# Two blocks on one core: small fp32 products of attention and scan in other groups, bias rows built early, four gate pairs as plain products

## The chip, the cores and the metric

One core of a Trainium2 chip runs the whole program in one launch. The metric is the time of one execution in device microseconds, as the median of several runs. The kernel before took 2028.05 us (three runs: 2022.07, 2028.05 and 2031.63 us). Matrix products run on TensorE (PE in the views, PEld is its weight load), elementwise work on VectorE (DVE) and ScalarE (ACT), small work and one DMA queue on GpSimd (POOL); most transfers are issued by SyncE (SP). Each engine works off its own instructions strictly in the order in which they were laid down.

## What is computed

A sequence of 1024 tokens of width 1024 passes through two blocks; everything is float32. Cut to what the change touches:

```python
h = rmsnorm(x, norm_mix_pre)
q, k, v, u, g_attn, g_ssm = split(h @ w_in)          # 512, 128, 128, 512, 1024, 1024
logits = q·k / 8 + bias[dist]                        # 8 query heads, 2 kv heads, blocks of 128
p = softmax over 256 keys and one sink               # the block itself and the one before it
y_attn = (p @ v) @ w_attn_branch
z = gelu(s5_ssm(u, lam, log_dt, b, c, d_skip))       # 32 groups of 16 channels, 64 complex states
z = z * sigmoid(z @ w_glu);  y_ssm = z @ w_ssm_branch
merged = sigmoid(g_attn) * y_attn + sigmoid(g_ssm) * y_ssm
x = x + rmsnorm(merged @ w_out)
x = x + rmsnorm(square(relu(rmsnorm(x) @ w_ff_in)) @ w_ff_out)
...
```

The lines left out are a second block with three branches and a last norm; the change does not touch its code.

## The kernel before

**Large products.** A float32 matrix is held as two float16 parts (`split`, L135 on ACT for the high part, L136 on DVE for the low part), and a product takes three float16 matmuls per slice of the contraction. Two column tiles of 128 are made at a time, a "pair". `strassen` makes a pair by seven products of 12 matmuls of 512 columns (L208 to L210), with four differences (`tw`, L164) and seven splits of weights ahead of it and an evacuation of one ACT copy (L226), two sums into `u` (L231, L237) and three into `c` or a destination (L253). `first_pair` makes a pair plainly: 96 matmuls (L383), four splits of weights, and an evacuation straight from PSUM. Weights come by SP in blocks `raw` of 512 KB (L145, three buffers) and are split into a pool of `NW` = 15 pairs of weight tiles `whi`/`wlo`.

**Order.** The program is written as units, each with a preparation (loads and splits of its weights) that is started some units earlier. A list scheduler of the framework lays the instructions of all units out on each engine by dependences and priorities. The order is fixed when the program is built.

**Startup.** Eight tiles of x are squared and summed on ACT (L540), the reciprocal root comes by way of DVE (L426) and POOL (L428, `rs`), DVE makes the normed rows `h` (L541), PE transposes them (`tr`, L448), and the transposed tiles are split. `first_pair` for k and v (`pq`) starts on the first tokens while later tiles are still on the way (its first half is cut in two pieces of 256 columns); the pair for the first half of q follows, then a `strassen` pair for the second half.

**Bias.** A unit behind the `strassen` pair of q (L573 to L592) multiplies a one-hot table with the copied bias table by eight fp32 matmuls `pbias` (K = 33, all 128 output rows alike, L586), copies them to 128 partitions, writes them to DRAM (`bdr`, 1.5 MB, L589) and reads them back with a row pitch one element short (L591), which gives each row its shift.

**Attention.** For each block of 128 tokens `attend` makes the logits `lg` (L773), a fused sum and maximum on DVE (L775), the exponentials on ACT (L784) and the scaling on DVE; `values` transposes the probabilities (`pt`, L800), copies them, and multiplies by v (`pvo`, L807: per block four groups, each of two matmuls with 256 columns that fill one half of the output rows). A fp32 matmul is two records in the trace.

**Scan.** For each of four groups of channels (`uc`) `ssm_tables` builds tables: `pwk` (L921, 16 output rows), one ACT copy of 16x512 for each half, DMAs by POOL, `pg` transposes (L934). `ssm_scan` makes the states `S` (L944), the scan on DVE, and the output `py`: for each half `a` and each `r` one product with K = 128 (L969) and then two with K = 64 (L971). The scan's u goes through DRAM (`udr`) into 16 partitions at a time by eight POOL DMAs of 256 KB (L985). Pairs of the two gates, GA and GS, are laid beside attention and scan as filler for PE.

**Parameters of the scan** (L625 to L757) are many small DVE operations on temporaries in the memory of the arena from 92 to 108 KB, which also holds the transposed tiles in float32 (`K32`).

Of the kernel before, what the change touches and what calls it, by code (L numbers as in the profile page):

```python
# [16 lines left out]
P = 128  # L17
T = 1024
D = 1024
H = 512  # L20
# [30 lines left out]
def kernel(ctx: ExitStack, tc: tile.TileContext, I: dict, out: bass.AP):  # L51
# [8 lines left out]
    R = 152  # L60
    NW, NQ = 15, 12
# [273 lines left out]
    def linear2(W, c0, act, cb, scale, early=None):  # L335
# [3 lines left out]
        def prepare():  # L339
            raw = load_k(W, lambda w: w.rearrange("(k p) n -> p k n", p=P), c0)  # L340
            for c in range(2):
                ws.append(hl_tile())
                split(*ws[c], raw[:, :, c * P:(c + 1) * P], SW)
# [180 lines left out]
    a21_1 = Flat(144)  # L524
    g_pre = A32(140, D)
    K32 = [A32(92 + 8 * q, 4 * H).rearrange("p (k t) -> p k t", k=4) for q in range(4)]

    @do
    def _():
        xin = [A32((72, 56)[t // 4] + 4 * (t % 4), D) for t in range(NT)]  # L530
        for t in range(NT):
# [3 lines left out]
            if t == 1:  # L535
                prepare(1)
# [22 lines left out]
    bias_t = A32(84, 8 * 256).rearrange("p (h s) -> p h s", h=8)  # L559
    sink = small([P, 8], "sink")  # L560

    @do
    def _():
        nc.vector.tensor_copy(kk[0:64, 1, :], kk[64:128, 0, :])
# [7 lines left out]

    @do  # L573
    def _():

        relb = small([33, 8], "relb")
        nc.vector.memset(relb, 1.0)
        nc.gpsimd.dma_start(out=relb[0:32, :], in_=I["rel_bias"])
        hot = A32(92, 384)[0:33, :]
        nc.gpsimd.dma_start(out=hot, in_=I["onehot"])  # L580
        relrep = A32(94, 8 * P)[0:33, :].rearrange("p (h m) -> p h m", h=8)
        nc.vector.tensor_copy(relrep, relb.unsqueeze(2).to_broadcast([33, 8, P]))
        vrow = A32(108, 8 * 384).rearrange("p (h i) -> p h i", h=8)
        for h in range(8):
            pb = aux("pbias")
            MM(pb[:, 0:384], relrep[:, h, :], hot, start=True, stop=True)  # L586
            nc.scalar.copy(vrow[:, h, :], pb[:, 0:384])
        bdr = pdr.tile([P, 8 * 384], F32, tag="bdr", name="bdr")
        nc.gpsimd.dma_start(out=bdr, in_=vrow.rearrange("p h i -> p (h i)"))  # L589
        skew = bass.AP(bdr.tensor, bdr.offset + 127, [[8 * 384 - 1, P], [384, 8], [1, 256]])  # L590
        nc.gpsimd.dma_start(out=bias_t, in_=skew)  # L591
        nc.gpsimd.dma_start(out=sink, in_=I["sinks"][0].partition_broadcast(P))  # L592
# [13 lines left out]
    toff = [92.0]  # L606

    def tmp(n):
        a = A32(toff[0], n)
        toff[0] += n * 4 / KB  # L610
        assert toff[0] <= 108
        return a
# [13 lines left out]
    def _():  # L626
        L16 = tmp(3 * P)[0:16, :].rearrange("p (i m) -> p i m", i=3)
# [8 lines left out]
        prm = tmp(48).rearrange("p (i r) -> p i r", i=3)  # L636
# [3 lines left out]
        def EXP(dst, src, n):  # L640
            save = toff[0]
# [15 lines left out]
        def SINCOS(sn, cs, y, n):  # L657
            save = toff[0]
# [34 lines left out]

        dt_ = small([P, 16], "dt")
# [13 lines left out]
        TT(Ai[:, 1, :], mags[:, 0, :], snd[:, 0, :], ALU.mult)  # L708
        for m in (1, 2, 4):
# [4 lines left out]
        nr, den, f_r, f_i, t1 = (tmp(16) for _ in range(5))  # L714
# [13 lines left out]
        braw = tmp(512).rearrange("p (i r c) -> p i r c", i=2, r=NP)  # L728
# [4 lines left out]
        tb1 = tmp(256).rearrange("p (r c) -> p r c", r=NP)  # L733
        tb2 = tmp(256).rearrange("p (r c) -> p r c", r=NP)
        cmul(Bf[:, 0], Bf[:, 1], frb, fib, braw[:, 0], braw[:, 1], tb1, tb2)
        for i, n_ in enumerate(("c_re", "c_im")):
            craw = tmp(256).rearrange("p (u q) -> p u q", u=4)
# [52 lines left out]
    def values(n):  # L790
        pr = Pb[n % 2]
        for kv in range(2):
            pv = aux("pvo")
            for par in range(2):
                pt = aux("pt")
                for i in range(2):
                    h = kv * 4 + par + 2 * i
                    for half in range(2):
# [192 lines left out]
    for c0 in range(0, 8, 2):  # L991
        gate_ahead(GS, c0)
# [533 lines left out]
```

## Time and profile before

| | before |
|---|---|
| median of three runs | 2028.05 us (2022.07 to 2031.63) |
| the profiled execution | 2025.8 us, its span 2024.1 us |
| PE busy | 1971.5 us (97%), 9536 matmuls |
| DVE busy | 1534.5 us (76%) |
| ACT busy | 875.8 us (43%) |
| POOL busy | 105.4 us (5%) |
| DMA | 171.80 MB, mean 85 GB/s |

The span is the time between the first and the last record; the execution's own time is 1.7 us above it. A matmul's busy time is modelled and overlaps with its neighbours: a matmul of 512 columns counts as about 380 ns though the next one starts 216 ns later. Gains on PE are therefore counted from one start to the next, which is what the timeline view gives. Idle time in the rows is put down to what ended it.

### The profile page before, as it was taken

What the parts mean: (1) busy time and instruction counts of PE and PEld (TensorE: products, weight loads), DVE (VectorE), ACT (ScalarE), POOL (GpSimd) and SP (SyncE); (2) the same over time, 40 slices, a digit from 0 to 9 for tenths busy, and PEclk for the clock granted to TensorE, in tenths of its full rate; (3) what the DMA queues carried; (4) which work ended last, traced back from release to release, by engine and by line L of the source; (5) the groups of instructions that cost most, each with busy time, mean ns of one, the idle gap of its engine ahead of it and who ended that gap; (6) DMA issues with size and microseconds to landing.
All of it is one profiled execution on the core that took longest, in us unless ns stands there. A gap on an engine that the chain in (4) does not pass through costs nothing. (4 is left out here: it accounts for less than half of the span.)

```text
span 2024.1 us, 25660 instructions
## 1 busy us (share of the span) xinstructions
PE 1971.5 (97%) x9536; PEld 938.3 (46%) x9536; DVE 1534.5 (76%) x2830; ACT 875.8 (43%) x1691; POOL 105.4 (5%) x157
## 2 busy tenths in 40 slices
PE   7999999999999999999999999999999999999998
PEld 5434445554454444444444444454444443444443
DVE  7687679877568966878876578589678896899942
ACT  7316643334246735625527445434333332344511
POOL 1000000110010000000000011000000011110000
PEclk9999999999999999999999999999999999999999
DMA  5231162577321221121122422211111121112222
GB/s 182 87 109 53 42 132 69 162 235 254 104 89 63 63 73 42 63 62 53 58 68 94 126 76 86 67 43 60 63 56 62 53 63 31 63 63 68 89 84 84
DMA packets 130574, 171.80 MB, mean 85 GB/s; under 512 B 12025, under 2 KB 98293, under 8 KB 130320
## 3 DMA queue, kind: packets, MB, share of 16 engines
q1 hardware_dynamic: 124736, 160.46, 24.4%
q0 software_dynamic: 3536, 8.64, 2.4%
q10 hardware_dynamic: 2176, 1.05, 0.3%
q8 instruction: 75, 1.23, 0.2%
q14 instruction: 51, 0.42, 0.1%
HBM read 138.01 MB, written 30.93 MB: 83 GB/s over the span
## 5 line engine op out<-in xcount | busy, mean ns | idle before, releaser
L208 PE MATMUL b<-arena,whi 128*128 128x512 f16 x2044 | 776.8, 380 | 9.1 <-ACT p L226 6.5
L209 PE MATMUL b<-arena,whi 128*128 128x512 f16 x2044 | 777.2, 380 | 0.9 <-DVE arena L136 0.9
L210 PE MATMUL b<-arena,wlo 128*128 128x512 f16 x2044 | 776.5, 380 | 0.0
L135 ACT ACTIVATE whi<-tw 128x512 f16<-128x512 f32 x292 | 172.9, 622 | 337.6 <-DVE tw L164 286.8
L209 PEld LDWEIGHTS <-whi 128*128 128x128 f16 x2044 | 200.5, 98 | 253.1 <-issue 19.8
L210 PEld LDWEIGHTS <-wlo 128*128 128x128 f16 x2044 | 200.5, 98 | 243.1 <-issue 7.6
L208 PEld LDWEIGHTS <-whi 128*128 128x128 f16 x2044 | 200.5, 98 | 242.6 <-issue 8.0
L253 DVE SCALAR_TENSOR_TENSOR c<-b,u 128x512 f32<-128x512 f32 x204 | 139.7, 686 | 109.9 <-PE b L210 109.6
L136 DVE SCALAR_TENSOR_TENSOR wlo<-tw,whi 128x512 f16<-128x512 f32 x292 | 194.2, 683 | 7.7 <-ACT whi L135 7.4
L136 DVE SCALAR_TENSOR_TENSOR wlo<-raw,whi 128x512 f16<-128x512 f32 (+1 forms) x261 | 176.7, 687 | 13.9 <-ACT whi L135 13.7
L415 PEld LDWEIGHTS <-arena 128*128 128x128 f16 x1152 | 112.7, 98 | 133.2
L135 ACT ACTIVATE whi<-raw 128x512 f16<-128x512 f32 (+1 forms) x261 | 151.2, 609 | 41.5 <-PE b L209 17.0
L164 DVE TENSOR_TENSOR tw<-raw,tw 128x512 f32<-128x512 f32 x134 | 91.8, 685 | 1.4 <-DMA raw<-in_w_in_dram 0.4
L843 ACT ACTIVATE c<-c 128x512 f32<-128x512 f32 x60 | 37.7, 629 | 116.6 <-DVE c L253 98.4
L354 PE MATMUL pl<-arena,whi 128*128 128x512 f16 x320 | 83.1, 379 | 2.2 <-DVE fetch L997 1.8
L415 PE MATMUL po<-arena 128*128 128x512 f16 x384 | 84.0, 379 | 0.0
L415 PE MATMUL pf<-arena 128*128 128x512 f16 x384 | 84.0, 379 | 0.0
L415 PE MATMUL pw<-arena 128*128 128x512 f16 x384 | 83.0, 379 | 0.0
L231 DVE SCALAR_TENSOR_TENSOR u<-b,p 128x512 f32<-128x512 f32 x79 | 54.0, 684 | 33.0 <-PE b L210 32.9
L383 PE MATMUL pq<-arena,whi 128*128 128x512 f16 (+1 forms) x288 | 79.0, 360 | 0.0
L237 DVE SCALAR_TENSOR_TENSOR u<-b,u 128x512 f32<-128x512 f32 x79 | 54.1, 685 | 17.6 <-PE b L210 17.5
L226 ACT ACTIVATE p<-b 128x512 f32<-128x512 f32 x79 | 46.0, 583 | 38.2 <-PE b L210 38.2
(326 smaller groups left out, 2175.5 us busy)
## 6 DMA issues: line engine op xcount, KB each, us to landing
raw<-in_w_in_dram SPq DMA_DIRECT2D x86, 512.0 KB, 3.5
raw<-in_w_ff_in_dram SPq DMA_DIRECT2D x32, 512.0 KB, 3.6
raw<-in_w_ff_out_dram SPq DMA_DIRECT2D x32, 512.0 KB, 3.5
fetch<-gdr SPq DMA_DIRECT2D x32, 256.0 KB, 4.2
xr<-xdr SPq DMA_DIRECT2D x32, 256.0 KB, 3.4
gdr<-c SPq DMA_DIRECT2D x24, 256.0 KB, 2.0
arena<-in_x_dram SPq DMA_DIRECT2D x8, 512.0 KB, 9.9
raw<-in_w_out_dram SPq DMA_DIRECT2D x8, 512.0 KB, 5.6
```

The costliest lines, as they stand in the source:

```text
L135: ACT(hi, src, AF.Copy, scale=scale)
L136: STT(lo, src, scale, hi, ALU.mult, ALU.subtract)
L164: TT(t, a, b, ALU.subtract)
L208: MM(b[:, 0:n], whi[:, k], act[0][:, i, k, sl], start=(first and k == 0), stop=False, skip_group_check=not first)
L209: MM(b[:, 0:n], whi[:, k], act[1][:, i, k, sl], start=False, stop=False, skip_group_check=not first)
L210: MM(b[:, 0:n], wlo[:, k], act[0][:, i, k, sl], start=False, stop=(k == nk - 1), skip_group_check=not first)
L231: STT(v["u2"], o2, scale, v["p1"], ALU.mult, ALU.add)
L237: STT(v["u3"], o, scale, v["u2"], ALU.mult, ALU.add)
L253: STT(d, vw(o), scale, vw(v[u]), ALU.mult, ALU.add)
L354: MM(bs[s], w[:, k], a[:, k, s * H:(s + 1) * H], start=(k == 0 and w is hi and a is act[0]), stop=(k == 3 and w is lo))
L383: MM(o, w[:, k % 4], a, start=(k == 0 and w is hi and a is ahi), stop=(k == 7 and w is lo))
L415: MM(bs[s], part(a), w[:, s * H:(s + 1) * H], start=(k == 0 and a is ahi and w is whi), stop=(k == nk - 1 and a is alo))
```

## The change

Six things change.

1. **Second gate.** The four pairs of GS are made by `first_pair` in place of `strassen`.
2. **Bias.** One `pbias` matmul with eight output rows takes the place of eight. Its unit becomes a function `bias_rows`, called in the startup behind the load of the second tile of x. The table goes to DRAM from 8 partitions, each row read 128 times (`to_broadcast`), and `bias_read` stands in the unit behind the k/v and q pairs.
3. **Room.** The arena grows from 152 to 160 KB, the weight tiles go from 15 to 11 pairs, and the temporaries of the scan's parameters move out of the memory of `K32`.
4. **values.** Per block four groups of four transposes, then four matmuls of 512 columns whose output rows alternate between the lower and the upper half, and one split of 128x512. The attention's output is ordered by kv head, so `linear2` loads `w_attn_branch` in two DMAs of 64 partitions.
5. **pwk.** The products go to four strips of 32 output rows in turn; four ACT copies of 16x128 take the place of one of 16x512.
6. **py.** All eight products with K = 128 come first, then sixteen with K = 64 that alternate between the row halves `a` = 0 and 1 and two PSUM banks.

```diff
-    R = 152
-    NW, NQ = 15, 12
+    R = 160
+    NW, NQ = 11, 12
...
+            if by_kv:
+                raw = pw.tile([P, 4, 256], F32, tag="raw", name=nm("raw"), bufs=3)
+                for a in range(2):
+                    nc.sync.dma_start(out=raw[64 * a:64 * a + 64],
+                                      in_=W[256 * a:256 * a + 256].rearrange("(k p) n -> p k n", p=64)[:, :, c0:c0 + 256])
...
+    def bias_rows():
...
+        hot, row = q2("hot"), q2("vrow")
+        nc.gpsimd.dma_start(out=hot[0:33, 0:384], in_=I["onehot"])
+        pb = aux("pbias")
+        MM(pb[0:8, 0:384], relb, hot[0:33, 0:384], start=True, stop=True)
+        nc.scalar.copy(row[0:8, 0:384], pb[0:8, 0:384])
+        nc.gpsimd.dma_start(out=bdr.rearrange("p (h i) -> h p i", h=8),
+                            in_=row[0:8, 0:384].unsqueeze(1).to_broadcast([8, P, 384]))
...
+    def bias_read():
+
+        skew = bass.AP(bdr.tensor, bdr.offset + 127, [[8 * 384 - 1, P], [384, 8], [1, 256]])
+        nc.gpsimd.dma_start(out=bias_t, in_=skew)
...
             if t == 1:
+                bias_rows()
                 prepare(1)
...
     @do
     def _():
+        bias_read()
         nc.vector.tensor_copy(kk[0:64, 1, :], kk[64:128, 0, :])
...
-    toff = [92.0]
...
+    toff = [131.0]
...
+        for half, kv in parts:
+            pt = aux("pt")
+            for i in range(4):
+                nc.tensor.transpose(pt[:, i * P:(i + 1) * P], pr[:, 4 * kv + i, half * P:(half + 1) * P], ident)
+            pts[half, kv] = A32(142 + 2 * (2 * half + kv), H)
+            nc.scalar.copy(pts[half, kv], pt)
+        pv = aux("pvo")
+        for half, kv in reversed(parts):
+            MM(pv[kv * 64:(kv + 1) * 64, :], vtok[:, n - 1 + half, kv * 64:(kv + 1) * 64], pts[half, kv],
+               start=(half == 1), stop=(half == parts[0][0]))
+        sl = (slice(None), slice(None), slice(n * P, (n + 1) * P))
+        split(at[0][sl], at[1][sl], v4(pv), SA)
...
+        if plain:
+            first_pair(w_in, col + c0 * P, hC, a21_1, cb, UNH)
...
+            for i in range(2):
+                for r in range(4):
+                    MM(pk[32 * r:32 * r + C, 0:P], Bf[rows, i, p0 + r, :],
+                       CA[rows, i, r, 0:8, :].rearrange("p d c -> p (d c)"), start=(i == 0), stop=(i == 1))
             for r in range(4):
-                for i in range(2):
-                    MM(pk[0:C, r * P:(r + 1) * P], Bf[rows, i, p0 + r, :],
-                       CA[rows, i, r, 0:8, :].rearrange("p d c -> p (d c)"), start=(i == 0), stop=(i == 1))
-            nc.scalar.copy(Wsb[:, :, a, :], pk[0:C, :].rearrange("p (r m) -> p r m", r=4))
+                nc.scalar.copy(Wsb[:, r, a, :], pk[32 * r:32 * r + C, 0:P])
...
+        for r in range(4):
+            for a in range(2):
+                MM(pys[a][:, cols_[r]], Kt[:, 2 * r + a, :], U[:, 2 * r + a, :], start=(r == 0), stop=False,
+                   skip_group_check=(r > 0))
+        for r in range(4):
+            for i in range(2):
+                for a in range(2):
+                    rows = slice(a * 64, (a + 1) * 64)
+                    MM(pys[a][:, cols_[r]], CA[rows, i, r, 1:9, :].rearrange("p d c -> p (d c)"), Ht[rows, i, r, :],
+                       start=False, stop=(i == 1), skip_group_check=(r > 0))
...
-        gate_ahead(GS, c0)
+        gate_ahead(GS, c0, True)
```

The units are written in another order at the startup, so the scheduler lays the engines' instructions out in another order there. On POOL the eight steps `rs` are the reciprocal roots of the eight tiles of x, in order. Before, behind the first of them:

```order
L428 TENSOR_TENSOR rs_24_141<-rs_24_141,mhalf_75 128x1
L428 TENSOR_TENSOR rs_28_163<-rs_28_163,mhalf_75 128x1
L428 TENSOR_TENSOR rs_32_185<-rs_32_185,mhalf_75 128x1
L428 TENSOR_TENSOR rs_36_207<-rs_36_207,mhalf_75 128x1
L428 TENSOR_TENSOR rs_40_229<-rs_40_229,mhalf_75 128x1
L428 TENSOR_TENSOR rs_44_251<-rs_44_251,mhalf_75 128x1
L428 TENSOR_TENSOR rs_48_273<-rs_48_273,mhalf_75 128x1
L746 DMA arena<-in_d_skip_dram 16x512
L580 DMA arena<-in_onehot_dram 33x384
```

And on POOL in the changed kernel, from the second tile's root on:

```order
L436 TENSOR_TENSOR rs_28_153<-rs_28_153,mhalf_75 128x1
L549 DMA bdr<-vrow_96 8x128x384
L436 TENSOR_TENSOR rs_32_175<-rs_32_175,mhalf_75 128x1
L436 TENSOR_TENSOR rs_36_197<-rs_36_197,mhalf_75 128x1
L556 DMA arena<-bdr 128x8x256
L436 TENSOR_TENSOR rs_40_219<-rs_40_219,mhalf_75 128x1
L436 TENSOR_TENSOR rs_44_241<-rs_44_241,mhalf_75 128x1
L436 TENSOR_TENSOR rs_48_263<-rs_48_263,mhalf_75 128x1
L436 TENSOR_TENSOR rs_52_285<-rs_52_285,mhalf_75 128x1
```

The write of `bdr` now stands between the roots of the second and the third tile, and its read back, which needs the write to have landed, in front of the roots of tiles five to eight.

On DVE, at the normed rows of the second and third tile (L541 before, L572 in the changed kernel), before:

```order
L541 SCALAR_TENSOR_TENSOR arena<-arena,rs_24_141 128x1024
L426 TENSOR_SCALAR rs_28_163<-ss_27_161 128x1
L541 SCALAR_TENSOR_TENSOR arena<-arena,rs_28_163 128x1024
L136 SCALAR_TENSOR_TENSOR arena<-tr_145,arena 128x4x128
L136 SCALAR_TENSOR_TENSOR arena<-tr_150,arena 128x4x128
L426 TENSOR_SCALAR rs_32_185<-ss_31_183 128x1
L541 SCALAR_TENSOR_TENSOR arena<-arena,rs_32_185 128x1024
```

And in the changed kernel, the last instructions up to the third tile's rows (`raw_477` to `raw_650` are the blocks of weights of the second half of q and of the pair behind it):

```order
L164 TENSOR_TENSOR tw_497<-raw_479,raw_477 128x512
L164 TENSOR_TENSOR tw_507<-raw_479,tw_487 128x512
L136 SCALAR_TENSOR_TENSOR wlo_490<-tw_487,whi_489 128x512
L136 SCALAR_TENSOR_TENSOR wlo_494<-tw_485,whi_493 128x512
L164 TENSOR_TENSOR tw_656<-raw_648 128x512
L164 TENSOR_TENSOR tw_658<-raw_650,tw_656 128x512
L164 TENSOR_TENSOR tw_668<-raw_650,raw_648 128x512
L164 TENSOR_TENSOR tw_678<-raw_650,tw_658 128x512
L572 SCALAR_TENSOR_TENSOR arena<-arena,rs_32_175 128x1024
L434 TENSOR_SCALAR rs_36_197<-ss_35_195 128x1
L572 SCALAR_TENSOR_TENSOR arena<-arena,rs_36_197 128x1024
```

The third tile's rows, and with them those of all later tiles, now stand behind work on six further blocks of weights, the last of which is the eighth block that the program loads.

On PE, the end of the eight products with K = 128 of the scan's output and the first of the others in the changed kernel (L981 has K = 128, L987 K = 64; before, one product of the first kind and two of the second alternated in one bank):

```order
L981 MATMUL py_2530<-arena 128x128
L981 MATMUL py_2531<-arena 128x128
L981 MATMUL py_2530<-arena 128x128
L981 MATMUL py_2531<-arena 128x128
L987 MATMUL py_2530<-arena 128x128
L987 MATMUL py_2531<-arena 128x128
L987 MATMUL py_2530<-arena 128x128
```

The products with K = 64 now follow one another in pairs that use different rows of the array and different banks.

## Rows read from the trace of the kernel before

**Rows 1.** The page: length of the span, busy time of PE and the others.
```profile
span 2024.1 us, 25660 instructions
...
PE 1971.5 (97%) x9536; PEld 938.3 (46%) x9536; DVE 1534.5 (76%) x2830; ACT 875.8 (43%) x1691; POOL 105.4 (5%) x157
```

**Rows 2.** Stretches: busy time and instructions of each engine, granted clock, DMA share.
```profile
core 0: us, PE busy (x) PEld busy (x) DVE busy (x) ACT busy (x) POOL busy (x), PEclk, DMA share, GB/s
50.00:100.00 50.00, 50.00 (x216) 23.29 (x214) 35.02 (x46) 19.21 (x31) 4.24 (x7) 0.93 0.27 90
90.00:100.00 10.00, 10.00 (x33) 4.27 (x32) 1.88 (x5) 2.03 (x4) 2.13 (x4) 0.67 0.39 159
...
200.00:250.00 50.00, 49.66 (x241) 25.07 (x241) 30.83 (x117) 28.18 (x83) 1.60 (x3) 1.00 0.10 34
...
350.00:400.00 50.00, 49.62 (x292) 29.70 (x291) 46.19 (x100) 18.90 (x35) 6.38 (x12) 1.00 0.59 158
...
1000.00:1050.00 50.00, 50.00 (x233) 22.69 (x232) 39.33 (x65) 13.31 (x25) 0.00 (x0) 1.00 0.21 63
```

**Rows 3.** Waits of PE: engine, line, waited for, us in total, times, longest.
```profile
PE tr L448 <- DVE arena L541: 13.9, 3, 7.9
...
PE lg L773 <- DVE m L775: 4.9, 2, 2.9
...
PE b L209 <- DVE arena L136: 0.9, 2, 0.4
```

**Rows 4.** Groups of PE by form: count | busy, mean ns | idle before.
```profile
L807 PE MATMUL pvo<-arena 128*64 128x256 f32 x120 | 32.8, 393 | 0.6
...
L921 PE MATMUL pwk<-arena 64*16 64x128 f32 x128 | 12.8, 270 | 0.0
...
L586 PE MATMUL pbias<-arena 33*128 33x384 f32 x16 | 6.9, 594 | 0.0
```

**Rows 5.** Timeline of PE in attention and scan: start, length of the run.
```profile
208.00 0.38 PE L209 MATMUL b<-arena,whi 128*128 128x512 f16 x1
208.21 0.38 PE L210 MATMUL b<-arena,wlo 128*128 128x512 f16 x1
208.52 1.08 PE L807 MATMUL pvo<-arena 128*64 128x256 f32 x4
209.53 0.39 PE L208 MATMUL b<-arena,whi 128*128 128x512 f16 x1
...
303.72 1.97 PE L944 MATMUL S<-arena 128*64 128x128 f32 x32
...
317.30 0.49 PE L969 MATMUL py<-arena 128*128 128x128 f32 x2
317.72 0.71 PE L971 MATMUL py<-arena 64*128 64x128 f32 x4
318.36 0.49 PE L969 MATMUL py<-arena 128*128 128x128 f32 x2
```

**Rows 6.** Costs on DVE: the page's groups of weight splits, differences and evacuations.
```profile
L253 DVE SCALAR_TENSOR_TENSOR c<-b,u 128x512 f32<-128x512 f32 x204 | 139.7, 686 | 109.9 <-PE b L210 109.6
...
L164 DVE TENSOR_TENSOR tw<-raw,tw 128x512 f32<-128x512 f32 x134 | 91.8, 685 | 1.4 <-DMA raw<-in_w_in_dram 0.4
```

**Rows 7.** Timeline of the startup on DVE, ACT and PE.
```profile
16.15 1.28 DVE L541 SCALAR_TENSOR_TENSOR arena<-arena,rs 128x1024 f32<-128x1024 f32 x1 [0.73 <-POOL rs L428]
...
12.82 1.05 ACT L540 ACTIVATE arena<-arena 128x1024 f32<-128x1024 f32 x1
...
35.81 0.59 PE L383 MATMUL pq<-arena,whi 128*128 128x512 f16 x2
```

**Rows 8.** DMA issues from 90 to 100 us: KB, us to landing.
```profile
bdr<-arena POOLq DMA_DIRECT2D x1, 1536.0 KB, 5.4
```

**Rows 9.** Waits of POOL.
```profile
POOL arena L591 <- DMA bdr<-arena: 4.6, 1, 4.6
```

**Rows 10.** DMA from 248 to 256 us: packets, the queue's share, issues with us to landing.
```profile
DMA packets 223, 0.78 MB, mean 98 GB/s; under 512 B 32, under 2 KB 32, under 8 KB 223
...
q0 software_dynamic: 223, 0.78, 84.6%
...
arena<-udr POOLq DMA_DIRECT2D x8, 256.0 KB, 12.0
raw<-in_w_in_dram SPq DMA_DIRECT2D x1, 512.0 KB, 21.3
```

**Rows 11.** The page's DMA issues: a block of weights over the whole program.
```profile
raw<-in_w_in_dram SPq DMA_DIRECT2D x86, 512.0 KB, 3.5
```

More of the change, by code (lines that the diff above doesn't have):

```diff
@@ L523 @@
     hC = COMB(0)
-    a21_1 = Flat(144)
+    a21_1 = Flat(152)
     g_pre = A32(140, D)
     K32 = [A32(92 + 8 * q, 4 * H).rearrange("p (k t) -> p k t", k=4) for q in range(4)]
+    bias_t = A32(84, 8 * 256).rearrange("p (h s) -> p h s", h=8)
+    sink = small([P, 8], "sink")
+    bdr = pdr.tile([P, 8 * 384], F32, tag="bdr", name="bdr")
+    def bias_rows():
+        relb = small([33, 8], "relb")
+        nc.vector.memset(relb, 1.0)
+        nc.gpsimd.dma_start(out=relb[0:32, :], in_=I["rel_bias"])
+        hot, row = q2("hot"), q2("vrow")
[5 more added lines that the diff above has]
+                            in_=row[0:8, 0:384].unsqueeze(1).to_broadcast([8, P, 384]))
+        nc.gpsimd.dma_start(out=sink, in_=I["sinks"][0].partition_broadcast(P))
+    def bias_read():
+        skew = bass.AP(bdr.tensor, bdr.offset + 127, [[8 * 384 - 1, P], [384, 8], [1, 256]])
+        nc.gpsimd.dma_start(out=bias_t, in_=skew)
     @do
@@ L571 @@
     strassen(w_in, 256, hC, nothing, UNH * 0.125, dest=lambda c, s, sl: q_t[:, 2 + c, s * H:(s + 1) * H])
[L573 to L592, printed above, removed]
     G, PS_, C = 32, 64, 16
@@ L605, with tmp @@
     mags = small([P, 2, 16], "mags")
-    toff = [92.0]
-    def tmp(n):
+    toff = [131.0]
+    def tmp(n, kb=None):
+        if kb is not None:
+            return A32(kb, n)
         a = A32(toff[0], n)
         toff[0] += n * 4 / KB
-        assert toff[0] <= 108
+        assert toff[0] <= 136
         return a
@@ L692, in SINCOS @@
             toff[0] = save
+        toff[0] = 135.0
         dt_ = small([P, 16], "dt")
@@ L708, in _ @@
         TT(Ai[:, 1, :], mags[:, 0, :], snd[:, 0, :], ALU.mult)
+        toff[0] = 131.0
         for m in (1, 2, 4):
@@ L713, in _ @@
                  Ar[:, m:m + 1, :].to_broadcast([P, m, 16]), Ai[:, m:m + 1, :].to_broadcast([P, m, 16]), t1, t2)
-        nr, den, f_r, f_i, t1 = (tmp(16) for _ in range(5))
+        toff[0] = 135.75
+        nr, den, f_r, f_i = (tmp(16) for _ in range(4))
+        t1 = tmp(16, 131)
         TS(nr, Ar[:, 1, :], -1.0, None, ALU.add)
@@ L791, in values @@
         pr = Pb[n % 2]
[L792 to L795, printed above, removed]
[L796 to L810 removed]
+        parts = [(half, kv) for half in range(0 if n else 1, 2) for kv in range(2)]
+        pts = {}
+        for half, kv in parts:
[10 more added lines that the diff above has]
+        split(at[0][sl], at[1][sl], v4(pv), SA)
     @do
@@ L963, in ssm_scan @@
         pys = [aux("py") for _ in range(2)]
[L964 to L972 removed]
+        cols_ = [slice(r * P, (r + 1) * P) for r in range(4)]
+        for r in range(4):
[8 more added lines that the diff above has]
+                       start=False, stop=(i == 1), skip_group_check=(r > 0))
+        for a in range(2):
             ACT(U.rearrange("p (r a) n -> p a r n", a=2)[:, a], pys[a].rearrange("p (r n) -> p r n", r=4),
```

51 lines of the change are left out of this document (15 added, 36 removed).

## The prediction

> **What bounds the kernel now.** I read the page first. PE is busy for 97% of the span [rows 1], so the time is PE's unless a stage shows otherwise. The table of stretches says where it is full: 216 to 233 instructions in 50 us where the matmuls have 512 columns, and 49.6 to 50 us busy also in attention (200 to 250 us) and scan (350 to 400 us) [rows 2]. There the count rises to 241 and 292: small fp32 products sit between the large ones. PE's waits are the third view: 4.9 us for the first logits, behind DVE, and 13.9 us for transposes at the startup, behind DVE's normed rows [rows 3]. So work taken from PE is time gained, if DVE and ACT keep up; the startup is the one stage in which PE waits for others.
>
> The sum is made against the profiled execution's 2025.8 us, which lies 2 us under the median of the runs. A difference under 0.5%, about 10 us, can't be told from none.
>
> **The bias product.** Eight matmuls become one. Their 16 records take 6.9 us [rows 4], in a stretch whose granted clock is 0.67, a mean of the two levels 1.2 and 2.4 GHz [rows 2]. Two records stay: **-6**.
>
> **values.** One group of four records takes PE from 208.52 to 209.53, 1.01 us, and its first record starts 0.31 us after the large matmul instead of 0.21 [rows 5]. Inside it, 256 columns take some 0.216 us a record, one after the other, since both matmuls use one half of the output rows. 120 records [rows 4] are 7.5 blocks of 16: 4.0 us a block. After, a block has 8 records of 512 columns, 0.43 us each, on alternating halves. What alternating halves do is seen at `S`: 32 records of 128 columns in 1.97 us with the tail, 62 ns each [rows 5], against 0.108 us for 128 columns alone (half the 0.216). Two run at a time. So 4 x 0.43 and a change, 1.9 us a block, 7.5 x 2.1 = **-16**. If they don't overlap it is -4.
>
> **pwk.** 128 records, 12.8 us [rows 4], 0.1 us each, so nothing overlaps now. Four strips of output rows take turns after. The nearest row is `S` with two halves: half the time, **-6**; between 0 and -9 (four at a time). The Trainium skill, "TensorEngine Tiling (Array Packing)", section "When to Use Tiling", has fourfold column tiling for 32 output rows. By it the term would be -9 and the sum 3 us lower; no row here has four strips. The added ACT copies (32 in place of 8, 128 columns each) lie beside PE: ACT is busy 19 of 50 us there [rows 2].
>
> **py.** One product with K = 128 and two with K = 64 take from 317.30 to 318.36, 1.06 us, for six records [rows 5]; of that 0.65 us would be six times 0.108, the rest are the two changes of tile shape. A `uc` has eight such, 8.5 us. After: 16 records at 0.108, 32 in pairs at 0.062, two changes at 0.1, 3.9 us. Four `uc` give **-18**; without overlap -12.
>
> **Fewer changes of shape elsewhere.** By the order of instructions PE changes between tile shapes 206 times in attention and scan now and 84 times after. About 25 of these are priced above; 100 at 0.09 us (the 0.31 against 0.21 us) are **-9**, between -4 and -11.
>
> **The gate.** Four pairs go from 84 to 96 matmuls: 48 x 0.216 = **+10**. DVE loses per pair four differences, three splits and five sums, 12 x 0.686 us [rows 6], 33 us in all. Its 46 of 50 us in the scan [rows 2] are work beside a full PE, so this gains nothing by itself; it is what lets a shorter PE be fed.
>
> **The parameters of the scan** leave the memory of `K32` and can run earlier, so part of the 4.9 us before the logits goes: **-3**, 0 to -5.
>
> **Tighter cover.** With 11 weight tiles in place of 15 a split waits for an older product's last matmul; before, PE waited only 0.9 us for splits [rows 3]. The weights of the branch come in two DMAs instead of one, loaded ahead. In attention, PE's shorter share brings it near the chain of DVE and ACT (28 of 50 us on ACT, 31 on DVE, a chain of several steps per block). I put **+7** on these together, 0 to +15.
>
> So far -41, and in steady state the change is a gain.
>
> **The startup** is what speaks against it. The write of `bdr` now reads from 8 partitions. Before, from 128 partitions, the same 1536 KB landed in 5.4 us [rows 8]. The nearest row for few partitions is the scan's load of u: 256 KB DMAs into 16 partitions each move 98 GB/s in all and land after 12 us [rows 10]. Eight partitions at half of that, 49 GB/s, give 1536 KB in 31 us. The lower bound is 5.4 us. I take 31, as the row nearest in form. The Trainium skill, "SBUF — State Buffer", on the DMA port swizzle, gives 27 GB/s a port and, for eight neighbouring partitions, two ports: 29 us, and a sum 2 us lower; that 16 partitions move 98 GB/s here agrees with it.
>
> The write starts when ACT has made the row, behind the square of the third tile, which starts at 12.82 [rows 7]: about 14.5 us. It lands at 46. Two things wait for it:
>
> - POOL waits for the landing before it reads the table back, as it did for 4.6 us before [rows 9]; now the roots of tiles five to eight are queued behind that wait. They come at 47 in place of 22 to 31 us.
> - Blocks of weights crawl beside such a transfer: one that came during the load of u took 21.3 us [rows 10], against 3.5 [rows 11]. DVE has the third tile's rows behind the eighth block. I have the third to fifth block landing between 25 and 46 us, then three more, each issued when a buffer is free, at about 2.5 us: the eighth at 50 to 56, the third tile's rows at 53 in place of 16.15 [rows 7].
>
> From there six rows of 1.28 us, splits between them and the last transposes take some 15 us, and all products with 512 columns stand behind the last transpose: 68 to 69 us in place of 35.81 [rows 7]. PE has only 10 us of pieces in between: **+33**, from +11 (quick write, then only the order on DVE delays, rows of tile three at 32) to +40.
>
> Sum: -6 - 16 - 6 - 18 - 9 + 10 - 3 + 7 + 33 = -8. **Forecast 2018 us**, on the edge of what can be told from no change; own range 2006 to 2034.
>
> **Rivals.**
>
> - *The write is not slow* (chance 0.18). It reads the same eight rows again and again and writes to DRAM, where the load of u wrote into SBUF; if it lands within 10 us, POOL's wait is over at 25 and the startup costs +11. For it: the 5.4 us of the same bytes. Against: the 98 GB/s. Time: 2018 - 22 = **1996**.
> - *The write is slower than in proportion, and PE starts later still* (0.12): slower than before. Place: POOL's wait in front of the root of tile five. If reads of one partition 128 times over come at 25 GB/s, 1536 KB take 62 us, it lands at 77, and the last transpose at 92: +56, **2041**. It is over the edge from a landing at 74 us on (a write of about 59 us).
> - *The regrouped products don't run two at a time* (0.08): the change then doesn't do what it says. Terms -4, 0 and -12 in place of -16, -6 and -18 add 24: **2042**. Against it stands `S`; for it, that K = 64 halves of the rows have no such clean row.
> - The rest (0.62) is the forecast's case.
>
> **How the numbers follow.** Within the forecast's case, +-10 around 2018 leaves about half under 2017.9 and nearly all the rest within 0.5%: faster 0.29, same 0.31, slower 0.02. The quick write adds 0.18 to faster; of the two slow rivals 0.16 are slower and 0.04 same. Faster 0.47, same 0.35, slower 0.18. For 8 in 10 the range takes the forecast's case, the quick write, and part of the slow rivals: 1993 to 2041.
>
> **What would show it.** In the profile after: the write of `bdr` issued near 14.5 us and landing in about 31; POOL waiting for it some 25 us; PE idle from about 25 to 53 us, its waits for `arena` of the normed rows up from 13.9 to 40 us or more; first 512-column matmul near 68. `pvo` records in pairs with starts a few ns apart and 1.9 us a block; `py` 3.9 us a `uc`; PE's busy time some 45 us lower. Wrong would be: a landing within 10 us (then 1996), idle of PE before `lg` or `pvo` over 20 us in sum, or busy times of `pvo` and `py` unchanged.

## The result and the profile after

The changed kernel takes **2050.12 us** (median of four runs, 2048.01 to 2054.67) against 2027.64 us for the kernel before, measured with it: a ratio of 1.0116, 95% interval 1.0099 to 1.0133. It is 22 us slower. The forecast was 2018 us, with a range from 1993 to 2041.

The profiled execution took 2048.01 us. Its page, the lines that answer to [rows 1]:

```profile
span 2046.3 us, 25718 instructions
...
PE 1943.8 (95%) x9510; PEld 917.0 (45%) x9510; DVE 1510.6 (74%) x2773; ACT 874.5 (43%) x1682; POOL 105.1 (5%) x157
```

PE is busy 28 us less and the span is 22 us longer, so PE stands idle some 50 us more. The waits of PE, the answer to [rows 3] (engine, line, waited for, us in total, times, longest), name most of it:

```profile
PE tr L456 <- DVE arena L572: 38.3, 5, 33.1
PE pwk L934 <- DVE arena L627: 8.6, 3, 3.4
PE pbias L547 <- DMA relb<-in_rel_bias_dram: 8.3, 1, 8.3
...
PE lg L787 <- DVE m L789: 3.5, 7, 1.3
...
PE b L209 <- DVE arena L136: 0.8, 2, 0.4
```

The transposes of the startup wait 38.3 us for the normed rows, 33.1 us of it in one piece; before, 13.9. The 8.3 us of `pbias` lie at the very start, where PE had nothing to do for 7.92 us before either. A wait of 8.6 us in the scan is new: `pwk` waits for a table that DVE makes.

**The startup.** The timeline of PE around the long wait, and its first product with 512 columns:

```profile
25.67 0.27 PE L391 MATMUL pq<-arena,wlo 128*128 128x256 f16 x1
59.06 1.94 PE L456 MATMUL tr<-ident,arena 128*128 128x128 f32 x8 [33.12 <-DVE arena L572]
...
76.08 1.24 PE L391 MATMUL pq<-arena,whi 128*128 128x512 f16 x5
```

POOL issues the write of `bdr` at 14.61 us. The view of DMA from 15 to 50 us:

```profile
DMA packets 3416, 5.11 MB, mean 146 GB/s; under 512 B 476, under 2 KB 2787, under 8 KB 3416
...
bdr<-vrow POOLq DMA_DIRECT2D x1, 1536.0 KB, 34.0
raw<-in_w_in_dram SPq DMA_DIRECT2D x2, 512.0 KB, 17.4
```

The write lands after 34.0 us where it took 5.4 [rows 8]. The 17.4 us are the mean of two very different blocks of weights, one issued at 22.61 us beside the write (28.2 us) and one at 45.40 near its end (6.7 us). The fourth and the fifth block were issued before this window, at 11.44 and 13.84 us, and were still on the way when the write began. The views of DMA from 10.5 to 12 us and from 12 to 20 us have their landings:

```profile
raw<-in_w_in_dram SPq DMA_DIRECT2D x1, 512.0 KB, 32.0
...
raw<-in_w_in_dram SPq DMA_DIRECT2D x1, 512.0 KB, 35.6
```

A block takes 3.5 us in the median of the whole program [rows 11], and 7.2 us in the median for those that the kernel before issued from 10 to 40 us. What DVE and ACT wait for from 10 to 60 us:

```profile
DVE wlo L136 <- ACT whi L135: 27.6, 3, 21.5
ACT whi L135 <- DMA raw<-in_w_in_dram: 27.3, 4, 21.6
...
DVE tw L164 <- DMA raw<-in_w_in_dram: 5.3, 2, 4.1
```

and the third tile's rows in its timeline:

```profile
57.64 1.28 DVE L572 SCALAR_TENSOR_TENSOR arena<-arena,rs 128x1024 f32<-128x1024 f32 x1
```

DVE waits 21.5 us in one piece for the split of the fourth block, which ACT cannot make before the block comes at 43.4 us, and works through the eighth block before it turns to the third tile at 57.64, in place of 16.15 [rows 7]. POOL shows which of the two waits named in the prediction ended last:

```profile
POOL rs L436 <- DVE rs L434: 59.3, 7, 41.3
...
POOL arena L556 <- ACT arena L135: 1.9, 1, 1.9
```

Its read of the table, L556, did not wait for the landing at all. It was reached only at 61.67, since the fourth root in front of it waited 41.3 us for DVE. The wait for the write was covered by the slower blocks of weights.

**The regrouped products** do what they should. PE's timeline in a block of attention and in one `uc` of the scan:

```profile
223.14 1.94 PE L817 MATMUL pvo<-arena 128*64 128x512 f32 x8
...
310.93 0.68 PE L934 MATMUL pwk<-arena 64*16 64x128 f32 x32
...
328.86 1.95 PE L981 MATMUL py<-arena 128*128 128x128 f32 x16
330.73 2.06 PE L987 MATMUL py<-arena 64*128 64x128 f32 x32
```

A block's `pvo` takes 1.94 us with its tail (4.0 before), a `uc`'s `py` 3.9 us (8.5 before), and 32 records of `pwk` take 0.68 us with their tail, 21 ns each against 0.1 us before [rows 4]: at least four at a time. **But PE is not full there any more.** The stretches, in the columns of [rows 2], first in the changed kernel and then in the kernel before:

```profile
150.00:200.00 50.00, 43.96 (x184) 21.34 (x182) 42.06 (x187) 21.62 (x68) 2.68 (x3) 0.83 0.22 71
...
300.00:350.00 50.00, 46.34 (x347) 24.52 (x346) 36.22 (x68) 19.36 (x41) 8.34 (x16) 0.97 0.39 102
350.00:400.00 50.00, 44.03 (x312) 24.35 (x310) 39.05 (x86) 12.30 (x26) 6.37 (x12) 0.97 0.42 106
```

```profile
150.00:200.00 50.00, 49.75 (x240) 24.03 (x239) 35.76 (x125) 31.16 (x101) 0.00 (x0) 1.00 0.16 54
300.00:350.00 50.00, 49.43 (x304) 27.64 (x303) 42.76 (x81) 15.05 (x25) 4.17 (x8) 1.00 0.22 65
```

From 350 to 400 us the kernel before had PE busy for 49.6 of 50 us at full clock as well [rows 2].

### The profile page after: what moved, and what is told of

It is laid out like the page before. It is cut to its first block, busy times and chain, and to the rows that moved or that the text cites. A ratio compares the mean times of both kernels' runs of the same rounds, so it can differ in the third digit from the quotient of the medians.

```text
span 2046.3 us, 25718 instructions
## 1 busy us (share of the span) xinstructions
PE 1943.8 (95%) x9510; PEld 917.0 (45%) x9510; DVE 1510.6 (74%) x2773; ACT 874.5 (43%) x1682; POOL 105.1 (5%) x157
## 5 line engine op out<-in xcount | busy, mean ns | idle before, releaser
L208 PE MATMUL b<-arena,whi 128*128 128x512 f16 x1932 | 732.9, 380 | 13.4 <-ACT p L226 6.7
L209 PE MATMUL b<-arena,whi 128*128 128x512 f16 x1932 | 733.5, 380 | 0.9 <-DVE arena L136 0.8
L210 PE MATMUL b<-arena,wlo 128*128 128x512 f16 x1932 | 732.3, 380 | 0.0
L209 PEld LDWEIGHTS <-whi 128*128 128x128 f16 x1932 | 189.3, 98 | 242.8 <-issue 20.6
L210 PEld LDWEIGHTS <-wlo 128*128 128x128 f16 x1932 | 189.2, 98 | 229.9 <-issue 5.6
L135 ACT ACTIVATE whi<-tw 128x512 f16<-128x512 f32 x276 | 165.4, 624 | 295.5 <-DVE tw L164 124.4
L208 PEld LDWEIGHTS <-whi 128*128 128x128 f16 x1932 | 189.2, 98 | 228.3 <-issue 4.4
L253 DVE SCALAR_TENSOR_TENSOR c<-b,u 128x512 f32<-128x512 f32 x192 | 131.3, 685 | 106.9 <-PE b L210 106.2
L136 DVE SCALAR_TENSOR_TENSOR wlo<-tw,whi 128x512 f16<-128x512 f32 x276 | 184.5, 682 | 13.0 <-ACT whi L135 12.8
L391 PE MATMUL pq<-arena,whi 128*128 128x512 f16 (+1 forms) x544 | 159.6, 376 | 0.6 <-ACT arena L135 0.3
L391 PE MATMUL pq<-arena,wlo 128*128 128x512 f16 (+1 forms) x272 | 101.9, 375 | 0.0
L391 PEld LDWEIGHTS <-whi 128*128 128x128 f16 x544 | 53.9, 100 | 58.1 <-issue 4.8
L853 ACT ACTIVATE c<-c 128x512 f32<-128x512 f32 x48 | 30.2, 629 | 85.1 <-DVE c L253 78.0
```

The lines of the kernel that those rows point to most:

```text
L135: ACT(hi, src, AF.Copy, scale=scale)
L136: STT(lo, src, scale, hi, ALU.mult, ALU.subtract)
L208: MM(b[:, 0:n], whi[:, k], act[0][:, i, k, sl], start=(first and k == 0), stop=False, skip_group_check=not first)
L209: MM(b[:, 0:n], whi[:, k], act[1][:, i, k, sl], start=False, stop=False, skip_group_check=not first)
L210: MM(b[:, 0:n], wlo[:, k], act[0][:, i, k, sl], start=False, stop=(k == nk - 1), skip_group_check=not first)
L253: STT(d, vw(o), scale, vw(v[u]), ALU.mult, ALU.add)
```

## The experiments

Ratios are to runs of the kernel before taken on the same chip with the kernel in question (median 2028.74, 2029.04, 2029.11 and 2030.35 us in the four sets). The first set asks which part of the change costs the time.

### The bias as before, all else as changed

```diff
-    bias_rows() at the second tile, bias_read() behind the first pairs
+    the unit of L573 to L592 of the kernel before, in its old place
```

> The changed kernel with the bias built as before: eight products, a write from 128 partitions, in its old place behind the pairs of q. Theory A (the write of the bias table from 8 partitions and the order around it cost the 40 us by which the first product of 512 columns is late, 76.08 us against 35.81, and nothing else depends on it): 512 columns start at 35 to 37 us, the eight products cost 5 to 7 us again, time 2050 - 40 + 6 = about 2016. Theory B (the later losses, 17 us of half clock from 163 to 180 us and the waits in the scan, follow from the late start as well): under 2000. Theory C (the attention and scan lose more when DVE must also keep up with an early start): over 2030.

Measured: 2014.24 us, ratio 0.9928 (0.9911 to 0.9946). This kernel is called bias_old below. The first product of 512 columns starts at 36.21 us. Theory A named 2016: the bias part costs 36 us of the changed kernel's time. The changed kernel's 17 us of half clock in attention, from 163 to 180 us, shrink to about 10 in two pieces, but the waits in the scan stay as they were, 8.6 us at `pwk`, so theory B does not hold for the waits.

### The bias part alone, on the kernel before

```diff
+    bias_rows() at the second tile, bias_read() behind the first pairs
-    the old bias unit
```

> The kernel before with the bias part of the change alone (early rows, write from 8 partitions, read behind the k/v and q pairs); 15 weight tiles, old products, old gate. Theory A: the first product of 512 columns starts at 74 to 78 us, the write lands in 33 to 35 us, time 2028 + 40 - 6 = about 2062. Theory B: more than 2075, with low clock in attention here too. If the time is under 2045, the late start is made up later and the loss lies in other parts.

Measured: 2079.25 us, ratio 1.0247 (1.0225 to 1.0270). The write lands in 34.9 us and 512 columns start at 78.34 us, as theory A says, but the time is 17 us above its 2062, and 51 us above the kernel before. So some loss comes later here, as theory B has it: its stretches from 350 us on have a granted clock of 0.86 and 0.83, where the kernel before had 1.00.

```profile
350.00:400.00 50.00, 49.76 (x265) 29.64 (x265) 40.20 (x84) 12.31 (x21) 6.38 (x12) 0.86 0.27 67
400.00:450.00 50.00, 46.38 (x244) 27.35 (x244) 39.65 (x77) 16.79 (x30) 4.15 (x8) 0.83 0.43 125
```

A mean clock 14% and 17% under full costs some 15 us of work in these two stretches, which is an estimate from the two rows and about the 17 us that theory A lacks. Why the clock fell there was not tried. So the bias part costs 36 us in the changed kernel and 51 us alone.

### The same bytes from 128 partitions

```diff
-        nc.gpsimd.dma_start(out=bdr.rearrange("p (h i) -> h p i", h=8),
-                            in_=row[0:8, 0:384].unsqueeze(1).to_broadcast([8, P, 384]))
+        nc.gpsimd.dma_start(out=bdr.rearrange("p (h i) -> p h i", h=8),
+                            in_=row[:, 0:384].unsqueeze(1).to_broadcast([P, 8, 384]))
```

> The changed kernel, but the write of the bias table takes the same 1536 KB from 128 partitions of one row tile (eight rows right, the others zero: the bias that attention adds is wrong here, its time is not). The scheduler also puts the normed rows of the third tile earlier. Theory A: the write lands in 5 to 7 us, blocks of weights are not slowed, 512 columns start at 36 to 42 us, time 2012 to 2020. Rival (the wait of POOL for any landing, whatever its length, holds the tiles up): start over 50 us, time over 2025.

Measured: 2016.54 us, ratio 0.9941 (0.9923 to 0.9959). The write lands in 9.9 us among the loads of the startup, the blocks issued from 10 to 40 us in 12.8 in the median, and 512 columns start at 40.86. POOL still reads the table back ahead of the roots of tiles five to eight, and that costs little: the rival falls. The write and the blocks are slower than theory A said (5 to 7 us, and blocks not slowed; the kernel before has 7.2 us for blocks issued then), without harm to the start. Since the scheduler also moved the third tile's rows forward, this run takes away the slow transfer and the late rows together.

### The same slow write, after the startup

```diff
-            if t == 1:
-                bias_rows()
...
+        bias_rows()
         bias_read()
```

> The changed kernel with one thing moved: the rows of the bias are built where they are read, behind the k/v and q pairs, so the same write from 8 partitions comes after the startup. Theory A (what costs is where the transfer lies: it slows the blocks of weights that the startup waits for): the write takes 32 to 36 us again, but begins at 36 to 45 us, when weights are split ahead; 512 columns start at 35 to 37 us; time 2008 to 2016, as with the old bias (2014), less 6 for the products, plus a few us for late weights. Rival (the slow transfer costs wherever it lies, since blocks of weights beside it need 15 to 20 us): PE waits for splits between 50 and 90 us, time 2025 to 2040.

Measured: 2036.68 us, ratio 1.0038 (1.0023 to 1.0054). This is the rival's number. The startup is back (512 columns at 36.04 us), DVE's order at the rows of the tiles is that of the kernel before, and the write is issued at 68.82 us, later than the 36 to 45 us expected, and takes 34.1 us. What DVE and PE wait for from 40 to 110 us, and the stretch from 75 us:

```profile
DVE tw L164 <- DMA raw<-in_w_in_dram: 24.7, 1, 24.7
...
PE b L208 <- DVE arena L253: 20.8, 1, 20.8
```

```profile
75.00:100.00 25.00, 9.59 (x45) 4.24 (x44) 2.45 (x4) 1.26 (x2) 0.00 (x0) 0.76 0.53 66
```

The two blocks issued beside the write take 32.1 and 26.5 us. DVE waits 24.7 us for one of them with an evacuation behind it in its order, and PE idles 20.8 us; it waits for that evacuation and not for a split, as the rival had it. So the slow transfer costs 22 us against bias_old with the order of the startup left alone, or some 28 if the shorter product saves the 6 us that [rows 4] let one expect: **the transfer alone costs time, by what it does to the loads beside it**. In the changed kernel the third tile's rows also stand behind these loads in DVE's order. No run has the slow write at the startup with the rows in their old place, or the late rows with a quick write, so how its 36 us divide between the two stays open.

### The second gate by Strassen again

```diff
-        gate_ahead(GS, c0, True)
+        gate_ahead(GS, c0)
```

> The changed kernel with the four pairs of the second gate by Strassen again. Theory D (the scan is bound by DVE's chain, pwk waits for DVE, and plain pairs only help): PE has 10 us less, but DVE 33 us more in a stretch where it is the one waited for; time 2050 to 2062, waits of pwk and S for DVE over 8.6 us. Rival (the plain pairs are simply 10 us of extra work): 2040, waits of pwk under 5 us.

Measured: 2041.04 us, ratio 1.0063 (1.0045 to 1.0080), 9 us faster than the changed kernel. `pwk` waits for DVE 8.6 us, exactly as with plain pairs. Theory D falls, and the rival has the time right but not the wait, which it put under 5 us: the lighter load on DVE buys nothing in the scan, and the plain pairs cost their 48 matmuls.

### The kernel before with 11 weight tiles

```diff
-    NW, NQ = 15, 12
+    NW, NQ = 11, 12
```

> The kernel before with 11 weight tiles in place of 15 and nothing else. Theory G (four tiles fewer hold splits back until a product is over, and PE waits): 2033 or more, PE waits for splits (L209, L208 from ACT or DVE) 5 us or more above before. Rival (the cover is enough): 2026 to 2031.

Measured: 2036.09 us, ratio 1.0042 (1.0029 to 1.0055), 7 us slower. Theory G in its size, but PE's waits for splits don't show it. It shows on ACT from 50 to 500 us:

```profile
ACT whi L135 <- PE b L209: 56.9, 27, 7.5
```

In the kernel before that line reads 6.7 us in 5 waits. ACT now waits for a product to end before it may overwrite a tile. PE is busy as before (1972.6 us against 1971.5) and idle for 58.1 us of its span in place of 52.6, spread over several waits; that these come from the splits on ACT is argued, not shown.

### The old py, pwk and values, one at a time

All three on bias_old (2014.24 us), so that the startup does not hide them. The first:

```diff
-        the eight products with K = 128, then sixteen that alternate
+        for a: for r: one product with K = 128, then two with K = 64, in one bank
```

> The kernel bias_old (2014 us) with the old order of the py products (K = 128 and K = 64 in turn, one bank). Theory E (PE sets the scan's pace): the regrouped py is worth its 18 us, time 2030 to 2034. Theory F (in the scan PE now waits for DVE's tables at pwk, 8.6 us, and a longer PE fills that wait): 2018 to 2026, waits of pwk for DVE under 4 us and fewer drops of the clock between 250 and 380 us.

Measured: 2024.64 us, ratio 0.9976 (0.9961 to 0.9991): the regrouped `py` is worth 10 us, not 18. Theory F. Undoing it makes PE 14.1 us longer busy (1961.4 against 1947.3 us). PE's waits from 250 to 400 us of bias_old:

```profile
PE pwk L934 <- DVE arena L627: 8.6, 3, 3.5
PE S L958 <- ACT arena L949: 1.4, 1, 1.4
PE pg L948 <- DVE arena L633: 0.9, 1, 0.9
PE pwk L934 <- DVE arena L631: 0.3, 1, 0.3
```

and with the old `py`:

```profile
PE S L958 <- ACT arena L949: 1.4, 1, 1.4
PE pg L948 <- DVE arena L627: 1.1, 1, 1.1
PE pg L948 <- DVE arena L633: 0.9, 1, 0.9
PE py L985 <- DVE arena L633: 0.5, 1, 0.5
PE pwk L934 <- DVE arena L631: 0.4, 2, 0.2
```

The wait of 8.6 us is gone when PE is longer. The stretch from 300 us has its full clock back, and PE is busy for 48.8 of 50 us:

```profile
300.00:350.00 50.00, 44.41 (x335) 23.45 (x336) 36.94 (x69) 15.35 (x36) 10.53 (x20) 0.97 0.44 98
```

```profile
300.00:350.00 50.00, 48.80 (x343) 26.61 (x343) 36.99 (x70) 16.00 (x37) 10.57 (x20) 1.00 0.39 90
```

The first row is bias_old, the second has the old `py`; DVE is busy 37 us in both. The second:

```diff
-            four strips of output rows in turn, four ACT copies
+            one strip, one ACT copy for each half
```

> The kernel bias_old (2014 us) with the old pwk (one strip of output rows, one ACT copy for each half). pwk goes from 3.5 us busy back to about 13. Theory E (PE sets the pace): 2021 to 2024. Theory F (pwk itself waits for DVE's tables, so its length comes on top of that wait and nothing is hidden): also 2021 to 2024, with 8 to 9 us of wait unchanged. If the time stays within 2011 to 2018, the four copies on ACT or the later tables eat what the four strips save.

Measured: 2019.11 us, ratio 0.9947 (0.9925 to 0.9969): worth 5 us, between the two ranges named. The interval overlaps that of bias_old (0.9911 to 0.9946), so the 5 us are hardly clear of noise. PE waits 7.2 us for DVE at `pwk` here too. The third:

```diff
-        values with four matmuls of 512 columns a block, linear2 by kv head
+        values with groups of two matmuls of 256 columns, linear2 as before
```

> The kernel bias_old (2014 us) with the old values (groups of two matmuls of 256 columns, 16 splits, attention's output by query head, w_attn_branch in one load). Theory E (PE sets the pace of attention): the regrouped values are worth 16 us, time 2028 to 2033. Theory F (the shorter PE waits for DVE and ACT there as in the scan): 2018 to 2025, with pvo back at about 33 us busy but fewer idle us before lg, pc and pt between 110 and 150 us.

Measured: 2031.45 us, ratio 1.0006 (0.9994 to 1.0018): worth 17 us, theory E. In attention PE did set the pace.

### Versions that join what paid

First, the changed kernel with the rows written once (12 KB) and spread from DRAM to DRAM, and the gate by Strassen:

```diff
-        nc.gpsimd.dma_start(out=bdr.rearrange("p (h i) -> h p i", h=8),
-                            in_=row[0:8, 0:384].unsqueeze(1).to_broadcast([8, P, 384]))
+        nc.gpsimd.dma_start(out=bd0.rearrange("o (h i) -> (o h) i", h=8), in_=row[0:8, 0:384])
+        nc.gpsimd.dma_start(out=bdr, in_=bd0.to_broadcast([P, 8 * 384]))
...
-        gate_ahead(GS, c0, True)
+        gate_ahead(GS, c0)
```

> A version that joins what paid: the changed kernel, but the bias rows go to DRAM once (12 KB from 8 partitions) and are spread there by a transfer from DRAM to DRAM, and the second gate is made by Strassen again. Theory A: the spread lands in 5 to 10 us, 512 columns start at 36 to 42 us as in write128, and the gate gives back 9 us (2050 to 2041 in the changed kernel): 2000 to 2010. Rival (two further landings for which POOL waits hold the tiles up as the slow write did): 512 columns start over 50 us, time over 2018.

Measured: 2005.83 us, ratio 0.9883 (0.9860 to 0.9906). The two transfers land in 4.8 and 7.1 us, and 512 columns start at 39.68.

```profile
bdr<-bd POOLq DMA_DIRECT2D x1, 1536.0 KB, 7.1
...
bd<-vrow POOLq DMA_DIRECT2D x1, 12.0 KB, 4.8
```

Second, the kernel before with the three regrouped products and nothing else:

```diff
     NW, NQ = 15, 12
...
+    values, pwk, py and linear2 by kv head as in the change
```

> The kernel before with the three regrouped products alone (values, pwk, py): 15 weight tiles, Strassen gate, old bias, parameters in their old place. If the parts add up as the runs so far give them (values -17, pwk -5, py -10; the tiles' +7 and the plain gate's +9 left out): 2029 - 32 = 1995 to 2000. Rival (the regrouped products need the plain gate's lighter load on DVE, since the scan then waits for DVE): 2005 to 2015, with waits of pwk for DVE over 12 us.

Measured: 2006.47 us, ratio 0.9881 (0.9863 to 0.9900), 24 us faster than the kernel before where the single parts add to 32. They are not additive. That all three shorten PE beside the same work of DVE would explain it; what is shown is that `pwk` waits for DVE 8.4 us here too, under the 12 of the rival, whose time it nevertheless has. This kernel is called regroup_only below. Third, the same with the bias spread in DRAM:

```diff
     regroup_only
+    bias_rows() at the second tile, written once and spread from DRAM to DRAM
-    the old bias unit
```

> The same with the bias rows built early and spread from DRAM to DRAM. The products' 6 us go, 512 columns start some 3 to 5 us later: 1993 to 2000, within 4 us of regroup_only. Rival (the early bias holds the tiles up): 2003 or more, 512 columns after 45 us.

Measured: **1999.72 us**, ratio 0.9851 (0.9837 to 0.9865), the fastest kernel of this study: 30 us under the kernel before and 50 under the changed one. 512 columns start at 40.54 us, and building the bias early is worth 7 us, just at the edge of the two intervals, once the table does not leave SBUF from 8 partitions 128 times.

## Why the prediction was wrong

The forecast had the sign wrong: 2018 us against 2050.12, outside its range. Two steps failed. The startup's loss had the right mechanism and was too small, and the step "so work taken from PE is time gained, if DVE and ACT keep up" failed in attention and scan: PE's work fell nearly as forecast, and less than half of it came out as time. The columns: the term as forecast, and what the runs give when that part alone is undone, the bias in the changed kernel and the others in bias_old or the changed kernel (the weight tiles: made alone on the kernel before).

| part | forecast us | runs us |
|---|---|---|
| bias: startup and products | +33 - 6 | +36 |
| values | -16 | -17 |
| pwk | -6 | -5 |
| py | -18 | -10 |
| changes of shape elsewhere | -9 | no part of its own |
| plain gate | +10 | +9 |
| parameters earlier | -3 | no part of its own |
| weight tiles, loads, chain | +7 | +7 (tiles) |
| sum | -8 | +20 |

The measured difference is +22. Of it two parts are measured as they stand together: the bias, +36 where +27 was forecast (+51 alone on the kernel before), and all the rest, bias_old against the kernel before, -14 where -35 was forecast. So 9 us of the miss lie in the bias and some 20 in the rest. That the rows of the rest add up so well, to -16, is in part chance: each carries 3 to 6 us of noise by the intervals, and `values`, `pwk` and `py`, -32 here, give only -24 together on the kernel before.

**PE's work and the time.** PE's line of bias_old's page, and its stretch from 100 to 480 us, the kernel before first, in the columns of [rows 2]:

```profile
PE 1947.3 (97%) x9524; PEld 918.9 (46%) x9524; DVE 1511.3 (75%) x2774; ACT 876.6 (44%) x1689; POOL 105.2 (5%) x157
```

```profile
100.00:480.00 380.00, 371.12 (x1934) 190.07 (x1934) 295.43 (x766) 158.29 (x352) 28.83 (x51) 1.00 0.45 125
100.00:480.00 380.00, 359.29 (x1977) 176.90 (x1976) 278.02 (x695) 161.25 (x364) 29.69 (x52) 0.97 0.47 130
```

PE is busy 24 us less than before [rows 1]. But some 20 of these 380 us are at the lower clock now, where eight transposes take 1.94 us instead of 1.06 (both at the startup of the changed kernel), so about 10 us of the busy time are lost to the clock. This is an estimate. At full clock PE's work is then some 34 us less, against 39 in the forecast's terms for it. The span, 2010.8 us, is only 13 us shorter: 10 us went to the clock, and PE's idle time grew by 11 us, from 52.6 to 63.5, most of it the 8.6 us at `pwk`. The forecast priced the waits at +7 and the clock at nothing. Its sign "PE's busy time some 45 us lower" shows the same in the changed kernel, where it is 28.

**The startup term** was right in kind and 7 to 8 us too small in time of start: 76.08 against the forecast's 68 to 69. Step by step: the write issued at 14.61 (14.5 forecast), landing in 34.0 us (31), the eighth block at 55.7 (50 to 56), the third tile's rows at 57.64 (53), and from there 18.4 us to the products with 512 columns (15). In the last step DVE waits three times 0.73 us for the root of a tile from POOL and 0.84 us for ACT, which the sum of rows and splits left out; the kernel before took 19.7 us for the same step (16.15 to 35.81).

```profile
59.83 1.28 DVE L572 SCALAR_TENSOR_TENSOR arena<-arena,rs 128x1024 f32<-128x1024 f32 x1 [0.73 <-POOL rs L436]
```

The granted clock was 0.50 from 30 to 59 us, while PE did nothing, and stayed low into the transposes:

```profile
30.00:59.00 29.00, 0.00 (x0) 0.00 (x0) 9.49 (x15) 2.93 (x5) 0.00 (x0) 0.50 0.46 89
```

DVE's waits for ACT behind these transposes are the 0.84 us, so the clock cost the path no more than that.

"POOL waits for the landing before it reads the table back" was not the step that ended last; the blocks of weights were, as the second point of the prediction had it. The -6 of the bias product is in the +36.

**The py term** is where the failed step shows best. DVE makes a `uc`'s tables behind the scan of the one before, and PE came to `pwk` three times 2 to 3.5 us too early. PE's own saving is as worked out, 8.5 us to 3.9 a `uc`; 10 of the 18 us came out as time. The prediction had called the plain gate "what lets a shorter PE be fed"; the run with Strassen pairs shows the same wait of 8.6 us.

**"Fewer changes of shape elsewhere are -9"** found hardly any room. Undoing `values`, `pwk` and `py` makes PE 15.7, 12.6 and 14.1 us longer busy, 42 in all, their changes of shape and some lower clock included, and the forecast has 40 for the three without this term. It should have stood in the range and not in the sum. Of the parameters of the scan no run gives the time; the wait before `lg` fell from 4.9 to 3.5 us, and to 1.8 in bias_old.

**The rivals.** "The write is slower than in proportion" named 2041, but its condition and its place are refuted: the write was near proportion (34.0 us for 8 partitions, 31 forecast), and POOL did not wait for its landing. "The regrouped products don't run two at a time", with 2042 the nearest in time, is refuted by the records of `pvo`, `pwk` and `py`. "The write is not slow" is refuted by the 34.0 us.

**The rules of the Trainium skill.** For the time of `pwk` on PE the -9 estimated from the Trainium skill, "TensorEngine Tiling (Array Packing)", "When to Use Tiling", was the better of the two prices: 12.8 us became 4.0. The time gained was still only 5. The port rule of the Trainium skill, "SBUF — State Buffer", on the DMA port swizzle, gave an estimate of 29 us for the write; the nearest row gave 31, and the run took 34.0.

## What to carry to other kernels

The transfer from 8 partitions took 34 us and, worse, held the loads beside it for 26 to 36 us, at the startup and later. Price such a transfer by what waits for those loads, and try spreading a small table in DRAM instead (4.8 and 7.1 us here). A saving on a full engine is a saving of time only until the next engine's chain is reached; look for what that engine waits for at the end of each stage and cap the term there; here a lower clock came on top. And where a change shrinks a pool of buffers for room, undo that alone first: four tile pairs cost 7 us, nearly half of what `values` gained.

## What the runs showed of the hardware

**The transfer from 8 partitions kept about half of the DMA engines busy and still delayed the loads beside it.** The changed kernel from 25 to 45 us, the queue's row (packets, MB, share of 16 engines' span):

```profile
q0 software_dynamic: 221, 1.02, 46.9%
q1 hardware_dynamic: 340, 0.33, 4.7%
```

The slow queue takes 46.9% of 16 engines, 7.5 of them. The Trainium skill, "DMA: Bandwidth & Descriptors", in "Why a DMA increments its semaphore by 16 and not by 1", says that a copy is split over the largest number of engines, up to 16, that divides the slowest dimension of both its sides, which here is 8; the 46.9% agree with it. The queue of the weights takes 4.7% and moves 0.33 MB in 20 us, though two to three blocks are on the way all the time, and the other engines stand idle. That the missing parts of these blocks lie behind the write on the engines that it holds would explain it; the trace does not say which engine a packet took, so this is argued. The slowest block took 35.6 us.

**Four strips of output rows run at least four at a time:** 21 ns a record for 128 columns, against 62 with two halves [rows 5] and 100 with one strip [rows 4].

**Short waits can be followed by half clock.** In bias_old PE waits 3.46 us for `pwk` until 329.57 and 3.23 us until 366.17 us. The stretches just behind, in the columns of [rows 2]:

```profile
330.00:333.40 3.40, 3.40 (x10) 0.93 (x8) 3.23 (x6) 0.00 (x0) 0.00 (x0) 0.51 0.80 187
...
367.60:371.00 3.40, 3.40 (x24) 0.99 (x23) 2.65 (x4) 2.12 (x7) 0.00 (x0) 0.50 0.00 0
```

The granted clock is at its lower level, 1.2 GHz, though PE is busy again. With the old `py` PE has no such wait there and full clock from 300 to 400 us. So each of these two waits cost some 1.7 us more than itself, an estimate from 3.4 us at half clock. It is no rule: after a wait of 3.43 us until 459.11 us in the version with the rows spread in DRAM and the gate by Strassen the clock stays full until 471 us, and the kernel with the bias part alone falls to half clock between 350 and 400 us with PE busy for 49.76 of 50 us.
